# A hybrid decoder block on one core: the merge's second operands split when they are loaded, its sums kept behind them, and scan transpositions placed inside the first product

## The chip, the core and the metric

The kernel runs on one core of one Trainium2 chip. The metric is the device time of one execution in microseconds (us). Before the change three runs took 1994.7, 1999.32 and 2001.35 us; their median is 1999.32 us.

## What is computed

The reference is a decoder block in float32 with 1024 tokens and 1024 channels. Two branches run in parallel: an attention with forget gates (FoX, 8 heads) and a gated delta rule (GDN, a chunked scan, 8 heads). Their outputs pass a projection each, are weighted by sigmoid gates and added, then follow an output projection, a gated feed-forward part with a short convolution, and a norm. The lines that matter here:

```python
o = gated_delta_rule(q, k, v, g, beta)
o = rmsnorm(o, gdn_norm[l]) * jax.nn.silu(gz.reshape(B, S, GDN_HEADS, GDN_HEAD_V))
y_gdn = o.reshape(B, S, GDN_V_WIDTH)

y = (jax.nn.sigmoid(gate_fox) * jnp.einsum('bse,ed->bsd', y_fox, w_branch_fox[l])
     + jax.nn.sigmoid(gate_gdn) * jnp.einsum('bse,ed->bsd', y_gdn, w_branch_gdn[l]))
h = h + jnp.einsum('bsd,de->bse', y, w_out[l])
```

## The kernel before

**Products in split precision.** A large product is not run on float32 operands. Each operand is split (`split`, L106 and L107) into a high part, a cast by ACT (`oh`, `yh`), and a low part, source minus high part, subtracted by DVE or POOL (`ol`, `yl`). `half_product` (L1654) then runs three matmuls for a pair: high by high, high by low, low by high. In `merge_split` (L1494) the weights become `oh` and `ol`, the activations `yh` and `yl`.

**The stages.** Projections of the input come first (to about 780 us). Then `mix` (L1285) runs the attention and the scan side by side: the attention's generator `fox` is advanced step by step, and two streams of scan heads (even heads, odd heads) are advanced in between. `merge` (L1513) follows, for branch 0 (FoX) and branch 1 (GDN), then the output projection (`mix_out`), the feed-forward part (`ffn_up`, `ffn_down`) and the output.

**The end of a scan head.** `columns(h)` (L1383) is a generator. Its first step loads the head's gate `sgz` and lets POOL scale the scan's output `so` (L1391 to L1396). Its next two steps each transpose four 128x128 blocks on PE (L1401), let ACT evict them into `yge` (L1405, for heads 6 and 7), let POOL multiply by the gate (L1406) and store the result in `ygd` (L1409). For head 6, the last of the even stream, these steps run inside the scan's end; head 7 is scaled last, and its transpositions stand in the middle of the merge's first product.

**The merge.** Each branch is one 1024x1024x1024 product, run as seven half-size products (a Strassen-Winograd scheme, the table `plan`, L1595). Each has four rounds k = 0 to 3, with 12 matmuls in a round. Rounds 0 and 1 run round by round, over the four column blocks i; rounds 2 and 3 then run block by block, so that the blocks end one after the other, and `after` works on each. The first product (n = 0) has operands `a11` and `b11`, which are split during the attention's end (`merge_first`, L1501). The second (n = 1) has `a12` and `b21`, loaded early into free buffers of the scan's inputs (`br_raw2`; in the trace they are named after these buffers: `skt`, `saq`, `sqd`, `skT` for k = 0 to 3). The splits of the second product are issued after `evicted`, the last eviction of `columns` (L1617). Each round of it also forms sums for later products (`sums2`, L1544): `b12 - b11` and `b22` minus that on DVE, `b22 - b12` on POOL. After each finished block, `gate` (L1522) loads the gate (L1525) and DVE weights the block with it (L1528).

**Order and buffers.** PE's order is the program's order. SP, ACT, DVE and POOL are ordered by a scheduler that works on a timeline of its own, except where the program pins an operation (`keep_in_program_order`) or ties it to another (`issue_after`). Each engine then works strictly in its order. Buffers are tiles of pools that are opened over memory that earlier pools gave up; an operation on a tile waits for the last use of what lay there. The gates' tiles `g` (four of 512 columns) lie in the pool `br2`, which `merge_gates` (L472) opens when the pool `so` (scan output, `sgz`, `yge`) is closed.

Of the kernel before, what the change touches and what calls it, by code (L numbers as in the profile page):

```python
# [9 lines left out]
F32 = mybir.dt.float32  # L10
# [57 lines left out]
def finish(gen):  # L68
    for _ in gen:
        pass  # L70
# [17 lines left out]
class Block:  # L88
# [322 lines left out]
    def run(self):  # L411
# [5 lines left out]
        with ExitStack() as ctx:  # L417
# [54 lines left out]
            def merge_gates():  # L472
                so.close()
                self.br.append(pool(bs, "br2"))

            def merge_second():
                si.close()
# [807 lines left out]
    def mix(self, fp, pool, before_last):  # L1285
        tc, nc, a = self.tc, self.nc, self.a
        self.yf_d, self.yg_d = ([self.dr.tile([P, S], F32, name=f"{n}{h}") for h in range(H)] for n in ("yfd", "ygd"))
        if True:
# [94 lines left out]
            def columns(h):  # L1383

                o, sumo = outs.pop(h)
                gz = self.so.tile([P, S], F32, tag="sgz", bufs=1, name="sgz")
                nc.sync.dma_start(gz, self.gz_d[h])
                f = self.rq[:, h, :]
                g_ = nc.gpsimd
                rs = self.so.tile([P, NB], F32, tag="srs", bufs=2, name="srs")  # L1390
                g_.tensor_tensor(rs, sumo, f, ALU.mult)  # L1391
                g_.tensor_tensor(rs, rs, f, ALU.mult)
                self.rsqrt(rs, rs, 1.0 / P, EPS)
                g_.tensor_tensor(rs, rs, f, ALU.mult)
                for sl in (slice(0, 4), slice(4, 8)):
                    g_.tensor_tensor(o[:, sl], o[:, sl], rs[:, sl].unsqueeze(2).to_broadcast([P, 4, P]), ALU.mult)  # L1396
                yield
                for g in range(2):
                    ps = self.small()
                    for j in range(4):  # L1400
                        nc.tensor.transpose(ps[:, j * P:(j + 1) * P], o[:, 4 * g + j, :], self.ident)  # L1401
                    y = self.so.tile([P, 512], F32, tag="yge", bufs=2, name="yge")
                    sl = slice(g * 512, (g + 1) * 512)
                    if h >= H - 2:
                        self.evicted = nc.scalar.activation(y, ps, AF.Copy, scale=self.gn[:, 0:1]).ins  # L1405
                        nc.gpsimd.tensor_tensor(y, y, gz[:, sl], ALU.mult)  # L1406
                    else:
                        nc.vector.scalar_tensor_tensor(y, ps, self.gn[:, 0:1], gz[:, sl], op0=ALU.mult, op1=ALU.mult)
                    nc.sync.dma_start(self.yg_d[h][:, sl], y)  # L1409
                    yield  # L1410
# [3 lines left out]
            def stream(s):  # L1414

                prev = iter(())
                for h in range(s, H, 2):
                    finish(preps.pop(h))
                    for i, _ in enumerate(scan(h)):
                        if i in (1, 6, 8):  # L1420
                            take(prev, 1)
                        if h + 2 < H and i in (14, 18, 21):
                            if i == 14:
                                preps[h + 2] = prep(h + 2)
                            take(preps[h + 2], 1)
                        yield
                    finish(prev)
                    prev = columns(h)
                if s == 0:
                    merge_loads(self.br_raw2, ("a12", "b21"), ("skt", "saq", "sqd"))  # L1430
                for _ in range(0 if s else 3):
                    take(prev, 1)
                    yield
                self.last.append(prev)

            def merge_loads(raw, names, tags):
# [33 lines left out]
            before_last()  # L1470
            for s in streams:
                finish(s)
            take(self.last[1], 1)


# [37 lines left out]
    def merge(self, gates_pool, second_pool):  # L1513
# [18 lines left out]
        for br in range(2):  # L1532
# [11 lines left out]
            def sums2(k):  # L1544
                b11, b12, b22 = (get(n, k) for n in ("b11", "b12", "b22"))
                t1 = b11 if br else temp(0, "b11")
                v.tensor_tensor(t1, b12, b11, subtract)
                b11 = blocks["b11", k] = t1
                t2 = blocks["t2", k] = temp(1, "t2")
                v.tensor_tensor(t2, b22, b11, subtract)  # L1550
                g.tensor_tensor(b12, b22, b12, subtract)
                if br == 0:

                    get("s2", k)
# [50 lines left out]
            for n, (wn, yn, tag, sums, after) in enumerate(plan):  # L1605
                fresh = n in (0, 1, 3)
                if fresh:
                    banks[tag] = [self.mm.tile([P, 512], F32, tag=tag, bufs=4, name=tag) for _ in range(4)]
                ps, last = banks[tag], []
                for k in range(4):  # L1610
                    if br == n == 0:
                        blocks["b11", k] = self.br_raw[k][:, 512:1024]
                        blocks["a12", k], blocks["b21", k] = (self.br_raw2[k][:, 512 * j:512 * (j + 1)] for j in range(2))
                        w, y = self.br_first.pop(0)
                    elif br == 0 and n == 1:

                        with self.tc.issue_after(self.evicted):  # L1617
                            w, y = self.merge_split(get(wn, k), get(yn, k), v)
                    else:
                        w, y = self.merge_split(get(wn, k), get(yn, k), v)  # L1620
                    if sums:
                        sums(k)
                    if k < 2:
                        for i in range(4):
                            self.half_product(ps[i], i, k, 4, y, w, fresh)
                    else:
                        last.append((k, 4, y, w, fresh))
                if br == n == 0:
# [466 lines left out]
```

## Time and profile before

| what | value |
| --- | --- |
| median of three runs | 1999.32 us |
| the profiled execution's own time | 2001.23 us |
| its span, first to last instruction | 1999.3 us |
| mean granted TensorE clock | 0.990 |
| PE busy, share of the span | 1923.4 us, 96% |
| DVE busy, share of the span | 1495.2 us, 75% |
| first, second and third product of the merge start at | 1072.1, 1084.1 and 1103.1 us |

A row of the timeline gives the start and the length in us, then the engine (PE matrix products, DVE, ACT and POOL the three vector engines, SPq SP's DMA issues), the line of the code, the operation, the tile written and the tiles read, the shape, and the count of merged instructions. Behind it, in brackets, stands how long the engine was idle just before, and what ended that. The lines of the code before are used throughout; behind the change they are higher by 2 to 6.

### The profile page before, as it was taken

The numbers are of one execution on the slowest core, as the hardware profiler recorded it, in microseconds if no ns is written. First come the engines' busy times: TensorE is split into PE (matmuls) and PEld (weight loads), VectorE is DVE, ScalarE is ACT, GpSimd is POOL, SyncE is SP. The second block draws the span as 40 slices with busy tenths as digits, with TensorE's granted clock in tenths as the row PEclk, the third lists the DMA queues.
The fourth block names the chain that finished last, engine by engine and source line by source line (L and its number), as shares of the span: only waits on it lengthen the run. The fifth ranks groups of instructions, "written<-read, shape, count | busy, mean of one in ns | idle before, by whom it ended". The sixth has DMA issues, their size and how long they took to land. (4 is left out here: it accounts for less than half of the span.)

```text
span 1999.3 us, 29171 instructions
## 1 busy us (share of the span) xinstructions
PE 1923.4 (96%) x9674; PEld 1609.2 (80%) x9674; DVE 1495.2 (75%) x2552; ACT 1067.3 (53%) x2383; POOL 938.7 (47%) x785
## 2 busy tenths in 40 slices
PE   8999999999999999899997999999999999999998
PEld 8988887788887877788886887877788888877886
DVE  6948888867999974487887797667876766778535
ACT  5436777763333455476765443466655555553234
POOL 2845656565554555465554033145656666530012
PEclk9999999999999999999999999999999999999999
DMA  5234556565323376767665933564433344378654
GB/s 170 92 108 160 176 190 185 182 217 195 122 99 107 111 227 252 216 222 233 212 215 172 317 107 121 183 228 153 152 117 132 132 132 137 103 247 322 222 191 162
DMA packets 191607, 350.88 MB, mean 176 GB/s; under 512 B 50784, under 2 KB 79712, under 8 KB 191456
## 3 DMA queue, kind: packets, MB, share of 16 engines
q1 hardware_dynamic: 189728, 344.04, 51.7%
q10 hardware_dynamic: 1728, 4.98, 0.6%
q8 instruction: 76, 1.25, 0.3%
q14 instruction: 75, 0.61, 0.1%
HBM read 232.76 MB, written 116.20 MB: 175 GB/s over the span
## 5 line engine op out<-in xcount | busy, mean ns | idle before, releaser
L107 POOL TENSOR_TENSOR ol<-ws,oh 128x512 fp32r<-128x512 f32 x212 | 290.6, 1373 | 217.2 <-ACT oh L106 206.9
L107 POOL TENSOR_TENSOR ol<-wr,oh 128x512 fp32r<-128x512 f32 x165 | 230.5, 1399 | 275.6 <-ACT oh L106 254.1
L106 ACT CAST oh<-ws 128x512 fp32r<-128x512 f32 x212 | 131.1, 618 | 176.6 <-PE mm L159 158.0
L205 DVE TENSOR_TENSOR ws<-wr 128x512 f32<-128x512 f32 x106 | 103.3, 974 | 98.8 <-DMA wr<-in_w_up_dram 73.1
L106 ACT CAST oh<-wr 128x512 fp32r<-128x512 f32 x201 | 121.4, 615 | 104.3 <-PE mm L159 72.0
L390 DVE SCALAR_TENSOR_TENSOR cv<-c,fw,cv 128x512 f32<-128x512 f32 (+2 forms) x176 | 127.5, 748 | 9.8 <-ACT cv L385 8.4
L390 DVE SCALAR_TENSOR_TENSOR cv<-c,cw,cv 128x511 f32<-128x511 f32 (+2 forms) x144 | 105.9, 747 | 7.8 <-ACT cv L385 6.3
L1044 DVE TENSOR_TENSOR invt<-invz 128x399 f32<-128x399 f32 (+50 forms) x114 | 95.0, 847 | 0.3
L264 ACT COPY x<-mm 128x512 f32<-128x512 f32 x158 | 91.8, 581 | 3.2 <-PE mm L159 3.2
L159 PE MATMUL mm<-b22h,oh 128*128 128x512 f32 x216 | 85.7, 397 | 5.9 <-ACT x L264 5.9
L159 PE MATMUL mm<-bt1h,oh 128*128 128x512 f32 x216 | 85.6, 396 | 4.3 <-ACT x L264 4.2
L159 PE MATMUL mm<-bt4h,oh 128*128 128x512 f32 x216 | 85.5, 396 | 3.4 <-DVE c L311 3.4
L107 DVE TENSOR_TENSOR ol<-wd,oh 128x512 fp32r<-128x512 f32 x66 | 45.5, 692 | 56.5 <-ACT oh L106 56.5
L159 PE MATMUL mm<-b11h,oh 128*128 128x512 f32 x216 | 85.9, 398 | 1.0 <-ACT oh L106 1.0
L159 PE MATMUL mm<-b11h,ol 128*128 128x512 f32 x216 | 85.9, 398 | 0.7 <-POOL ol L107 0.7
L159 PE MATMUL mm<-bt4l,oh 128*128 128x512 f32 x216 | 86.1, 399 | 0.0
L159 PE MATMUL mm<-b11l,oh 128*128 128x512 f32 x216 | 85.9, 398 | 0.0
L159 PE MATMUL mm<-b21l,oh 128*128 128x512 f32 x216 | 85.8, 397 | 0.0
L159 PE MATMUL mm<-b22l,oh 128*128 128x512 f32 x216 | 85.6, 396 | 0.0
L159 PE MATMUL mm<-bt2l,oh 128*128 128x512 f32 x216 | 85.1, 394 | 0.3 <-DVE bt2l L107 0.3
L159 PE MATMUL mm<-b21h,oh 128*128 128x512 f32 x216 | 85.2, 394 | 0.0
L159 PE MATMUL mm<-bt4h,ol 128*128 128x512 f32 x216 | 85.2, 394 | 0.0
(455 smaller groups left out, 6371.5 us busy)
## 6 DMA issues: line engine op xcount, KB each, us to landing
wr<-in_w_up_dram SPq DMA_DIRECT2D x43, 512.0 KB, 3.7
wr<-in_w_gdn_dram SPq DMA_DIRECT2D x24, 512.0 KB, 3.7
wr<-in_w_out_dram SPq DMA_DIRECT2D x24, 512.0 KB, 4.0
s<-z SPq DMA_DIRECT2D x44, 256.0 KB, 3.7
wd<-in_w_down_dram SPq DMA_DIRECT2D x44, 256.0 KB, 5.8
b22h<-s SPq DMA_DIRECT2D x44, 256.0 KB, 3.0
b22l<-s SPq DMA_DIRECT2D x44, 256.0 KB, 3.3
s<-hy SPq DMA_DIRECT2D x41, 256.0 KB, 3.0
```

The lines of the kernel that those rows point to most:

```text
L106: cast = nc.scalar.copy(hi, src)
L107: (lo_eng or nc.vector).tensor_tensor(lo, src, hi.bitcast(F32), ALU.subtract)
L159: self.nc.tensor.matmul(ps, lhs[:, sl], rhs[:, k, :], start=(first and k == 0 and i == 0), stop=(k == 3 and i == 2), skip_group_check=True)
L205: v.tensor_tensor(t, x, y, op)
L264: nc.scalar.copy(t, x)
L390: nc.vector.scalar_tensor_tensor(t[:, lo:], c[:, 512 * j + lo - s:512 * (j + 1) - s], w[:, n - 1 - s:n - s], t[:, lo:], op0=ALU.mult, op1= ...
L1044: nc.vector.tensor_tensor(tv, z[:, m:n, 0:n].to_broadcast([P, r, n]), z[:, m, c0:c1].unsqueeze(2).to_broadcast([P, r, n]), ALU.mult))
```

## The change

It has four parts.

1. Head 6's transpositions leave the scan. The even stream now only takes the first step of `columns` at its end (the scaling). The two transposing steps are taken inside the merge's first product, after blocks 1 and 3 of its first two rounds; head 7's stay where they were, behind round 1.
2. The second product's four splits are issued together, ahead of its rounds, and no longer tied to `evicted`.
3. In branch 0 the sums `b12 - b11` of DVE are pinned into program order, which is behind those splits.
4. A tile `gap` of 6 x 512 columns is put in front of the gates' tiles in their pool, so that these lie 12 KB further on. Nothing reads or writes it.

```diff
             def merge_gates():
                 so.close()
                 self.br.append(pool(bs, "br2"))
+
+                self.br[2].tile([P, 6 * 512], F32, name="gap")
...
                     if h >= H - 2:
-                        self.evicted = nc.scalar.activation(y, ps, AF.Copy, scale=self.gn[:, 0:1]).ins
+                        nc.scalar.activation(y, ps, AF.Copy, scale=self.gn[:, 0:1])
                         nc.gpsimd.tensor_tensor(y, y, gz[:, sl], ALU.mult)
...
                 if s == 0:
                     merge_loads(self.br_raw2, ("a12", "b21"), ("skt", "saq", "sqd"))
-                for _ in range(0 if s else 3):
+                if s == 0:
                     take(prev, 1)
-                    yield
                 self.last.append(prev)
...
                 t1 = b11 if br else temp(0, "b11")
-                v.tensor_tensor(t1, b12, b11, subtract)
+                ins = v.tensor_tensor(t1, b12, b11, subtract)
+                if br == 0:
+
+                    self.tc.keep_in_program_order(ins)
...
                 ps, last = banks[tag], []
+                early = []
+                if br == 0 and n == 1:
+                    early = [self.merge_split(get(wn, k), get(yn, k), v) for k in range(4)]
                 for k in range(4):
                     if br == n == 0:
...
                         w, y = self.br_first.pop(0)
-                    elif br == 0 and n == 1:
-
-                        with self.tc.issue_after(self.evicted):
-                            w, y = self.merge_split(get(wn, k), get(yn, k), v)
                     else:
-                        w, y = self.merge_split(get(wn, k), get(yn, k), v)
+                        w, y = early.pop(0) if early else self.merge_split(get(wn, k), get(yn, k), v)
                     if sums:
                         sums(k)
                     if k < 2:
                         for i in range(4):
                             self.half_product(ps[i], i, k, 4, y, w, fresh)
+                            if br == n == 0 and i % 2:
+                                take(self.last[0], 1)
```

What this makes of the order on the engines is shown at three places. Numbers behind a name tell its buffers apart.

DVE at the merge's start, before: `b11` written is the sum `b12 - b11`, `t2` the sum from it, `ol` and `yl` are the low parts of the second product's weights and activations (`skt` for k = 0, `saq` for k = 1, `sqd` for k = 2, `skT` for k = 3).

```order
L1547 TENSOR_TENSOR b11_12180<-b12_12074,skT_11623 128x512
L1547 TENSOR_TENSOR b11_12207<-b12_12076,skt_11626 128x512
L1547 TENSOR_TENSOR b11_12234<-b12_12078,saq_11629 128x512
L1547 TENSOR_TENSOR b11_12249<-b12_12080,sqd_11632 128x512
L107 TENSOR_TENSOR ol_12173<-skt_11889,oh_12172 128x512
L1550 TENSOR_TENSOR t2_12182<-b22_12082,b11_12180 128x512
L107 TENSOR_TENSOR yl_12177<-skt_11889,yh_12176 128x512
L107 TENSOR_TENSOR ol_12200<-saq_11892,oh_12199 128x512
L1550 TENSOR_TENSOR t2_12209<-b22_12084,b11_12207 128x512
L107 TENSOR_TENSOR yl_12204<-saq_11892,yh_12203 128x512
```

The same place of DVE after the change:

```order
L107 TENSOR_TENSOR yl_12178<-skt_11889,yh_12177 128x512
L107 TENSOR_TENSOR yl_12186<-saq_11892,yh_12185 128x512
L107 TENSOR_TENSOR yl_12194<-sqd_11895,yh_12193 128x512
L107 TENSOR_TENSOR yl_12202<-skT_12004,yh_12201 128x512
L1549 TENSOR_TENSOR b11_12205<-b12_12056,skT_11623 128x512
L107 TENSOR_TENSOR ol_12174<-skt_11889,oh_12173 128x512
L1555 TENSOR_TENSOR t2_12207<-b22_12064,b11_12205 128x512
L1549 TENSOR_TENSOR b11_12224<-b12_12058,skt_11626 128x512
L107 TENSOR_TENSOR ol_12182<-saq_11892,oh_12181 128x512
L1555 TENSOR_TENSOR t2_12226<-b22_12066,b11_12224 128x512
```

The four activation splits now stand first and one sum stands ahead of the first weight split, where four stood. Behind these rows follow, after the change, two more `b11` and two more `t2`, then `ol` of `sqd` and `ol` of `skT`, then `ol` of the third product's first `s2`; before it was the same set in another order, and the same `ol` of `s2` behind it.

ACT from the attention's last output on, before: `yge` is the eviction of four transposed blocks, `z` the copy of a finished block of the first product.

```order
L1249 COPY ye_12019<-ya_11839 128x512
L1379 ACTIVATE sjk_12016,sumo_11254<-so_11253 128x128
L1251 DMA yfd7_8364<-ye_12019 128x512
L1405 ACTIVATE yge_12123<-ms_12118,gn_542 128x512
L1405 ACTIVATE yge_12132<-ms_12127,gn_542 128x512
L106 CAST oh_12172<-skt_11889 128x512
L106 CAST yh_12176<-skt_11889 128x512
L106 CAST oh_12199<-saq_11892 128x512
L106 CAST yh_12203<-saq_11892 128x512
L106 CAST yh_12230<-sqd_11895 128x512
L106 CAST yh_12245<-skT_12022 128x512
L1566 COPY z00_12044<-a_12090 128x512
```

ACT at the same place after the change:

```order
L1253 DMA yfd7_8364<-ye_12001 128x512
L1407 ACTIVATE yge_12087<-ms_12082,gn_542 128x512
L106 CAST yh_12177<-skt_11889 128x512
L106 CAST yh_12185<-saq_11892 128x512
L106 CAST yh_12193<-sqd_11895 128x512
L106 CAST yh_12201<-skT_12004 128x512
L106 CAST oh_12173<-skt_11889 128x512
L1407 ACTIVATE yge_12102<-ms_12097,gn_542 128x512
L106 CAST oh_12181<-saq_11892 128x512
L1571 COPY z00_12026<-a_12072 128x512
L1407 ACTIVATE yge_12123<-ms_12118,gn_542 128x512
```

The second product's activation casts now stand behind the first eviction of head 6 (`yge_12087`) where they stood behind both of head 7. POOL's order changes with it: head 6's first gating (L1406) now stands behind the small steps and ahead of the scaling (L1396) of head 7, head 6's second behind that scaling, and head 7's two gatings behind the four subtractions `b22 - b12` (L1551), where all four gatings stood ahead of these. On SP the eight loads of `b12` and `b22` follow directly on the loads of `skT`; the load of `sgz` for head 7 and three of the four stores of `yge` stand behind those and behind six loads of weight sums.

DVE in `ffn_down`, at its first product, before; the scheduler's order there differs too, though no code of it was touched. `wd` written is a sum of weights that waits for a load, `ol` and `yl` are the low parts of round 6 and those after it.

```order
L2027 TENSOR_SCALAR nfin_18709<-nfin_18709 128x1024
L107 TENSOR_TENSOR yl_18753<-hr_18750,yh_18752 128x512
L1878 TENSOR_TENSOR wd00_0_18238<-wd0512_0_18742,wd00_0_18238 128x512
L107 TENSOR_TENSOR ol_18747<-wd00_6_18744,oh_18746 128x512
L1878 TENSOR_TENSOR wd00_1_18277<-wd0512_1_18770,wd00_1_18277 128x512
L107 TENSOR_TENSOR yl_18779<-hr_18750,yh_18778 128x512
L107 TENSOR_TENSOR ol_18775<-wd00_7_18772,oh_18774 128x512
L1878 TENSOR_TENSOR wd00_2_18305<-wd0512_2_18796,wd00_2_18305 128x512
L107 TENSOR_TENSOR yl_18807<-hr_18804,yh_18806 128x512
L1878 TENSOR_TENSOR wd00_3_18656<-wd0512_3_18824,wd00_3_18656 128x512
L107 TENSOR_TENSOR ol_18801<-wd00_8_18798,oh_18800 128x512
```

The same place after the change:

```order
L107 TENSOR_TENSOR yl_18754<-hr_18751,yh_18753 128x512
L2033 TENSOR_SCALAR nfin_18710<-nfin_18710 128x1024
L107 TENSOR_TENSOR ol_18748<-wd00_6_18745,oh_18747 128x512
L1884 TENSOR_TENSOR wd00_0_18239<-wd0512_0_18743,wd00_0_18239 128x512
L107 TENSOR_TENSOR yl_18780<-hr_18751,yh_18779 128x512
L1884 TENSOR_TENSOR wd00_1_18278<-wd0512_1_18771,wd00_1_18278 128x512
L107 TENSOR_TENSOR ol_18776<-wd00_7_18773,oh_18775 128x512
L1884 TENSOR_TENSOR wd00_2_18306<-wd0512_2_18797,wd00_2_18306 128x512
L107 TENSOR_TENSOR yl_18808<-hr_18805,yh_18807 128x512
L107 TENSOR_TENSOR ol_18802<-wd00_8_18799,oh_18801 128x512
L1884 TENSOR_TENSOR wd00_3_18657<-wd0512_3_18825,wd00_3_18657 128x512
```

The low part `ol` of round 8 stands ahead of the sum `wd00_3` where it stood behind it, and that of round 6 ahead of `wd00_0`. On ACT the load of `nfin` is issued two casts later.

## The prediction

> **What bounds the kernel now.** I read the page, then a table of windows over the merge, then PE, DVE and POOL in order of time through its first two products.
>
> ```profile
> span 1999.3 us, 29171 instructions
> ...
> PE 1923.4 (96%) x9674; PEld 1609.2 (80%) x9674; DVE 1495.2 (75%) x2552; ACT 1067.3 (53%) x2383; POOL 938.7 (47%) x785
> ```
>
> PE is busy for 96% of the span, so an edit that removes no matmul can only win PE's gaps and its slow stretches. The windows (busy us and count for each engine, granted clock, DMA share, GB/s) show where they lie:
>
> ```profile
> 1060.00:1066.00 6.00, 2.46 (x17) 1.81 (x15) 4.48 (x9) 3.58 (x11) 4.40 (x7) 1.00 0.27 94
> ...
> 1084.00:1090.00 6.00, 0.48 (x3) 0.05 (x1) 6.00 (x6) 1.76 (x4) 4.88 (x3) 0.80 0.72 270
> 1090.00:1096.00 6.00, 5.92 (x17) 4.72 (x18) 6.00 (x12) 1.14 (x2) 0.00 (x0) 0.63 0.00 0
> ...
> 1120.00:1140.00 20.00, 20.00 (x88) 16.19 (x87) 12.97 (x21) 10.34 (x19) 0.00 (x0) 1.00 1.04 383
> ```
>
> From 1120 on PE is full, so whatever the merge's start wins reaches the end. Before it PE stands twice, and once its clock falls to 0.63:
>
> ```profile
> 1065.60 0.66 PE L1401 MATMUL ms<-ident,so 128*128 128x128 f32 x4 [3.54 <-POOL so L1396]
> ...
> 1072.10 0.74 PE L1659 MATMUL a<-yp,oh 128*128 128x512 f32 x2 [0.68 <-ACT ye L1249]
> ...
> 1077.72 1.03 PE L1401 MATMUL ms<-ident,so 128*128 128x128 f32 x8
> ...
> 1084.08 0.40 PE L1659 MATMUL b<-yh,oh 128*128 128x512 f32 x1
> 1090.08 0.80 PE L1659 MATMUL b<-yl,oh 128*128 128x512 f32 x1 [5.60 <-DVE yl L107]
> ...
> 1091.10 0.63 PE L1659 MATMUL b<-yh,oh 128*128 128x512 f32 x1
> 1091.53 0.63 PE L1659 MATMUL b<-yl,oh 128*128 128x512 f32 x1
> ...
> 1094.72 0.40 PE L1659 MATMUL b<-yh,oh 128*128 128x512 f32 x1
> 1094.95 0.40 PE L1659 MATMUL b<-yl,oh 128*128 128x512 f32 x1
> ...
> 1103.12 0.40 PE L1659 MATMUL a<-yh,oh 128*128 128x512 f32 x1
> ```
>
> The first product starts at 1072.10, the second at 1084.08, the third at 1103.12. A matmul takes 0.23 us (1094.72 to 1094.95) and 0.43 while slow (1091.10 to 1091.53). The second product's 48 matmuls need 11.2 us, so of its 19.0 us 5.6 are the stall and some 2.0 the slow clock.
>
> ```profile
> 1067.90 1.00 DVE L1510 TENSOR_TENSOR ol<-sqd,oh 128x512 fp32r<-128x512 f32 x1
> ...
> 1079.19 1.82 DVE L1547 TENSOR_TENSOR b<-b,skT 128x512 f32<-128x512 f32 x1 [9.36 <-DMA b<-yfd]
> ...
> 1086.02 1.74 DVE L107 TENSOR_TENSOR ol<-skt,oh 128x512 fp32r<-128x512 f32 x1
> ...
> 1089.35 0.68 DVE L107 TENSOR_TENSOR yl<-skt,yh 128x512 fp32r<-128x512 f32 x1
> 1089.95 0.68 DVE L107 TENSOR_TENSOR ol<-saq,oh 128x512 fp32r<-128x512 f32 x1
> ...
> 1094.77 0.68 DVE L107 TENSOR_TENSOR ol<-skT,oh 128x512 fp32r<-128x512 f32 x1
> ```
>
> ```profile
> 1064.50 2.04 POOL L1396 TENSOR_TENSOR so<-so,srs 128x512 f32<-128x512 f32 x2
> 1067.06 1.30 POOL L1406 TENSOR_TENSOR yge<-yge,sgz 128x512 f32<-128x512 f32 x1 [0.52 <-ACT yge L1405]
> ...
> 1072.43 0.20 POOL L1391 TENSOR_TENSOR srs<-sumo,rq 128x8 f32<-128x8 f32 x1 [1.49 <-ACT sjk L1379]
> ...
> 1075.29 2.04 POOL L1396 TENSOR_TENSOR so<-so,srs 128x512 f32<-128x512 f32 x2
> 1079.17 2.99 POOL L1406 TENSOR_TENSOR yge<-yge,sgz 128x512 f32<-128x512 f32 x2 [1.84 <-DMA b<-yfd]
> 1082.12 6.75 POOL L1551 TENSOR_TENSOR b<-b,b 128x512 f32<-128x512 f32 x4
> ```
>
> DVE is what the second product waits for: idle for 9.36 us, then four sums ahead of any split. Until POOL's last subtraction ends (1088.87) each of DVE's operations takes about 1.75 us, afterwards one starts every 0.60. POOL's take 1.69 there (6.75/4) against 1.30. The two take turns: 0.60 for DVE, 1.09 for POOL.
>
> **The change, step by step.**
>
> *Start of the first product.* Head 6's transpositions leave the scan. Gone from PE are the 3.54 and 0.8 for eight transpositions (1077.72's eight, started within 0.8): 4.3 us. Next late is DVE: the last two splits of the attention's end, L1510 for `sqd`, move up into POOL's scaling of 1064.50 and stand ahead of an attention split that PE needs. If each waits for one half of the scaling (1.02), 4.3 - 2.0 = 2.3 us remain; if not, 4.3. I take 2.3, since the split at 1067.90 did wait for the gating at 1067.06 (1.00 for 0.68). Start: 1069.8.
>
> [...]
>
> *The first product.* It took 12.0 us with eight transpositions and takes 12.8 with sixteen. After 24 matmuls and eight transpositions (5.6 + 0.8) PE wants head 7's, at 1076.2. POOL's small steps for it took 2.9 (1072.43 to 1075.29), now from 1070.1 to 1073.0; then come one gating, now ahead of the scaling, and two halves (1.3 + 2.04), with DVE's splits between (two or three at 0.6, less the pause between operations, 0.2 each): 1077.5. The second half is wanted at 1076.6, so PE waits about 0.9. The second product starts at 1069.8 + 12.8 + 0.9 = 1083.5, only 0.6 earlier.
>
> *Operands of the second product.* ACT's four casts stand behind the first eviction, which needs head 6's transpositions (1.4 into the product), so the first `yl` comes at 1073.0, not when its load has landed. From there DVE has 16 operations: four `yl`, then sums and `ol`. POOL offers ten in that time (four gatings and four subtractions at 1.09, two scalings at 0.8): 10.3 us. The last `ol` but one, k = 2, is the fifteenth: 1073.0 + 14 x 0.60 + 10.3 = 1091.7, ready at 1092.4. `ol` of k = 0 is the sixth and is ready at about 1081.6, before 1083.5; that of k = 1 is the ninth, ready at 1086.7 where PE wants it at 1083.5 + 14 x 0.233 = 1086.8. So the 5.60 goes, but at matmul 27 (1089.6) PE waits until 1092.4: 2.8 to 3.0 us for `ol` of k = 2. Another 22 matmuls (5.1) and the third product starts at 1097.7. Against 1103.12 that is **-5.4**; the old order, worked through in the same way, comes out 0.1 early, so -5.3.
>
> *The clock after that stall.* An earlier stall of that size:
>
> ```profile
> 782.43 0.39 PE L1194 MATMUL ms<-kl,qh 128*128 128x256 f32 x1 [2.76 <-POOL kl L1142]
> ...
> 783.98 0.63 PE L159 MATMUL mm<-b11h,ol 128*128 128x512 f32 x1
> 784.40 0.63 PE L159 MATMUL mm<-b11h,oh 128*128 128x512 f32 x1
> ...
> 786.54 0.63 PE L159 MATMUL mm<-b11h,ol 128*128 128x512 f32 x1
> ```
>
> Seven matmuls at 0.43 follow it: 7 x 0.195 = 1.4 us. After the 3.54 at 1065.60 none do (they stand 0.23 apart). I take **+1.4**, bounds 0 and 2.0 (what followed the 5.60).
>
> [...]
>
> *Moved without a price.* SP's loads of `b12` and `b22`, and how long a gate's load takes to land:
>
> ```profile
> 1072.83 5.92 SPq L1484 DMA_DIRECT2D b<-yfd  x8
> ```
>
> ```profile
> DMA to landing us min/median/max: 2.5/3.0/4.8
> ```
>
> The eight loads no longer queue behind head 6's stores, which wait for POOL; they can go once the scan's buffers are free, some 5 us earlier, so DVE's 9.36 us wait for them goes too (its sums now come at 1079 anyway). Head 7's `sgz` load and its stores lie behind them, waiting for POOL; behind those stand the gates' loads, whose buffers moved onto `sgz` and `yge`. POOL's last gating ends at about 1089.4, its store lands at about 1092.4 if it takes the 3.0 of a gate's load. The gates' loads wait anyway for the split of the first `s2`, the operation after the last `ol`, at about 1093.7. That covers it by 1.3 us: 0, at worst +0.5. Without that cover each us is one on L1528 and on the splits behind it in DVE's queue.
>
> *The last stage.* There the order shifts by itself, as the scheduler works it out anew. DVE, PE and ACT before:
>
> ```profile
> 1791.90 0.69 DVE L2027 TENSOR_SCALAR nfin<-nfin 128x1024 f32<-128x1024 f32 x1 [3.08 <-DMA nfin<-in_norm_final_dram]
> ...
> 1801.29 0.69 DVE L1878 TENSOR_TENSOR wd<-wd,wd 128x512 f32<-128x512 f32 x1 [0.98 <-DMA wd<-in_w_down_dram]
> 1801.89 0.68 DVE L107 TENSOR_TENSOR ol<-wd,oh 128x512 fp32r<-128x512 f32 x1
> ```
>
> ```profile
> 1800.01 0.62 ACT L106 CAST oh<-wd 128x512 fp32r<-128x512 f32 x1 [8.31 <-DMA wd<-in_w_down_dram]
> ```
>
> ```profile
> 1802.63 0.50 PE L1659 MATMUL a<-ol,yh 128*128 128x512 f32 x1 [1.45 <-DVE ol L107]
> ```
>
> `ol` of k = 8 now precedes the sum that waits for its load, so it need not start at 1801.89 but once its high part is cast, at 1800.7: **-1.2**, bounds +1 (`nfin`, loaded two casts later, holds DVE longer than its 3.08) and -1.45 (the whole wait).
>
> *Sum*, against the profiled execution's 2001.23 (span 1999.3): 2001.23 - 5.3 + 1.4 - 1.2 = 1996.1. The median lies 1.9 below that execution, so 1994.2, or 0.26% under 1999.32.
>
> **Rivals.** *The clock stays full*, as after 1065.60: -5.3 - 1.2 = -6.5, 1992.8. For it: one stall of 3.54 without harm; against: 782.43. Chance 0.22.
>
> *The scalings exclude no split*: the first product starts at 1067.8 and ends without a wait at 1080.6; DVE's last splits come 3.6 earlier, the wait for k = 2 is 2.1, the third product starts at 1093.9: -9.2 - 1.2, about 1989. Against it 1067.90, which though was beside a gating. Chance 0.12.
>
> *Slower: the gates wait for the scan's last store.* If head 7's store of `yge` lands at L, the second gate lands 3.0 later and L1528 runs then; four operations behind it stands the split that the third product wants for k = 2, ready at L + 6.1. PE wants it at 1104.7 (1099.1 after the slow clock, plus 24 matmuls), so from L = 1098.6 on each us costs one, and such a stall the slow clock again (2.0). At L = 1103 that is +4.4 + 2.0 against -5.1: 2000.6. It turns slower from L = 1101.7. For it: the gates' loads have these waits now, and two casts, one load and one store of head 7 stand one behind the other. Against it: my 1092.4. Chance 0.05.
>
> *The splits gain nothing* because DVE is as late as before (`ol` of the last k at 1094.77): only start and `yl` are won, 2 to 3 us, 1996 to 1997. Chance 0.11.
>
> **How the numbers follow.** The forecast, 0.50: 1994.2, its own range 1992 to 1997. A measurement of this kernel (1994.7 to 2001.35 in three runs) can tell about 0.3%, 6 us, from no change, and the forecast lies just inside. Faster by more: nearly all of the second rival, somewhat over half of the first, and what of the forecast the spread carries over, 0.40. Slower by more needs the slow rival and the spread, 0.05. The rest, 0.55. The range 1990.0 to 1998.8 leaves out most of the second rival and the slow one.
>
> **What would show it.** Right: no PE wait on POOL's `so` before the first product; its start 2 to 4 us earlier; `yl` from about 1073; no 5.60 stall, in its place 2 to 4 us inside the second product for `ol`, with DVE at 1.7 beside POOL; the third product 4 to 5 us earlier. Wrong: a first product that ends later than 1084, an `ol` of k = 0 after the second product's start, a wait of DVE for gates above 1 us, or a last stage that shifts by more than 2 us.

## The result: 0.993 of the time before, a larger gain than forecast

Six runs of the changed kernel have a median of 1985.36 us (1982.76 to 1988.31), six of the kernel before 1999.16 us. The ratio is 0.9931, interval 0.9911 to 0.9951: 13.8 us less, where the forecast said 5.1 and its range ended at 1990.0. A second set gave 0.9944 (0.9926 to 0.9961), some 11.2 us less (0.0056 of 1998.2, the median of before over that set). The sign and, in sum, the merge's start came as forecast; a gain of 4 us at the other end of the merge, which the forecast set at 0, did not.

### The profile after

The first lines of the page:

```profile
span 1986.4 us, 29173 instructions
...
PE 1923.4 (97%) x9674; PEld 1610.1 (81%) x9674; DVE 1490.3 (75%) x2552; ACT 1066.8 (54%) x2383; POOL 940.8 (47%) x785
```

PE is busy for the same 1923.4 us, and its granted clock is 0.989 for 0.990: what this profile is shorter by is waiting. PE in order of time, from the attention's last score matmul (1044.12, called A below; it lies ahead of all that the change touches) to the third product:

```profile
1044.12 0.40 PE L1197 MATMUL ms<-kh,ql 128*128 128x512 f32 x1
...
1063.56 0.43 PE L1223 MATMUL ya<-pl,vh 128*128 128x256 f32 x1 [1.77 <-DVE pl L107]
...
1066.15 1.22 PE L1665 MATMUL a<-yp,oh 128*128 128x512 f32 x2 [0.68 <-ACT ye L1251]
...
1074.73 1.03 PE L1403 MATMUL ms<-ident,so 128*128 128x128 f32 x8
...
1081.09 0.40 PE L1665 MATMUL b<-yh,oh 128*128 128x512 f32 x1
...
1088.59 0.50 PE L1665 MATMUL b<-yh,ol 128*128 128x512 f32 x1 [0.95 <-DVE ol L107]
...
1090.27 0.50 PE L1665 MATMUL b<-yh,ol 128*128 128x512 f32 x1 [0.71 <-DVE ol L107]
...
1096.32 0.39 PE L1665 MATMUL a<-yh,oh 128*128 128x512 f32 x1
```

The 3.54 us for `so` and the 5.60 for `yl` are gone. In their place stand 1.77 for the attention's last `pl`, and 0.95 and 0.71 for `ol`. Head 7's eight transpositions (1074.73) waited for nothing. DVE at the same place:

```profile
1060.75 0.97 DVE L1512 TENSOR_TENSOR ol<-sqd,oh 128x512 fp32r<-128x512 f32 x1
1061.65 1.52 DVE L1512 TENSOR_TENSOR yp<-sqd,yp 128x512 fp32r<-128x512 f32 x1
1063.10 0.41 DVE L107 TENSOR_TENSOR pl<-ms,ph 128x256 fp32r<-128x256 f32 x1
1071.20 1.38 DVE L107 TENSOR_TENSOR yl<-skt,yh 128x512 fp32r<-128x512 f32 x1 [7.70 <-ACT yh L106]
...
1077.70 0.68 DVE L107 TENSOR_TENSOR ol<-skt,oh 128x512 fp32r<-128x512 f32 x1
...
1086.76 1.78 DVE L107 TENSOR_TENSOR ol<-sqd,oh 128x512 fp32r<-128x512 f32 x1
1088.46 1.75 DVE L107 TENSOR_TENSOR ol<-skT,oh 128x512 fp32r<-128x512 f32 x1
```

The prediction's working goes from the third product straight to the last stage. Between them, at the end of the merge, where the output projection (`mm`) begins, a wait has gone that it does not mention. PE, ACT and POOL there, before:

```profile
1237.46 0.40 PE L1659 MATMUL b<-yh,ol 128*128 128x512 f32 x1
1241.62 1.22 PE L1651 MATMUL mm<-oh,yh 128*128 128x512 f32 x2 [3.76 <-ACT yh L106]
```

```profile
1241.06 0.51 ACT L106 CAST yh<-z 128x384 fp32r<-128x384 f32 x1 [8.55 <-POOL z L1530]
```

```profile
1235.66 5.36 POOL L1530 TENSOR_TENSOR z<-z,g 128x512 f32<-128x512 f32 x4 [3.29 <-DVE g L1528]
```

And after:

```profile
1229.19 0.39 PE L1657 MATMUL mm<-oh,yh 128*128 128x512 f32 x1
1231.25 0.50 PE L1657 MATMUL mm<-oh,yh 128*128 128x512 f32 x1 [1.67 <-DVE g L1530]
```

```profile
1223.51 0.51 ACT L106 CAST yh<-z 128x384 fp32r<-128x384 f32 x1
```

```profile
1227.18 5.63 POOL L1532 TENSOR_TENSOR z<-z,g 128x512 f32<-128x512 f32 x4 [3.28 <-DVE g L1530]
```

The cast of the projection's first operand waited 8.55 us, until POOL's last addition of a gate had ended (1241.02). Its source had been finished earlier: after the change the same cast runs 3.7 us before POOL's last four additions begin, and waits for nothing. PE stood 3.76 us and went on at half clock (granted 0.50 from 1241.62 to 1244.60, 1.22 us for two matmuls); now it stands 1.67 and goes on at full clock (granted 1.00 from 1231.25 to 1234.00, 0.62 us for two).

### The profile page after: what moved, and what is told of

It reads as the page before. It is cut to its first block, busy times and chain, and to the rows that moved or that the text cites. A ratio compares the mean times of both kernels' runs of the same rounds, so it can differ in the third digit from the quotient of the medians.

```text
span 1986.4 us, 29173 instructions
## 1 busy us (share of the span) xinstructions
PE 1923.4 (97%) x9674; PEld 1610.1 (81%) x9674; DVE 1490.3 (75%) x2552; ACT 1066.8 (54%) x2383; POOL 940.8 (47%) x785
## 5 line engine op out<-in xcount | busy, mean ns | idle before, releaser
L205 DVE TENSOR_TENSOR ws<-wr 128x512 f32<-128x512 f32 x106 | 96.0, 906 | 107.2 <-DMA wr<-in_w_up_dram 72.7
L159 PE MATMUL mm<-bt1l,oh 128*128 128x512 f32 x216 | 85.4, 395 | 0.0
```

The source lines that it names most:

```text
L159: self.nc.tensor.matmul(ps, lhs[:, sl], rhs[:, k, :], start=(first and k == 0 and i == 0), stop=(k == 3 and i == 2), skip_group_check=True)
L205: v.tensor_tensor(t, x, y, op)
```

## The experiments

Each kernel left one profile. Since one program's executions differ by some us before A already (A lies between 1042.41 and 1048.87 in all profiles), the table counts from A: to the first product, from start to start of the products, from the third product to the output projection, and from there to PE's last matmul. The ratio is to the kernel before on the same chip.

| kernel | A to 1st | 1st to 2nd | 2nd to 3rd | 3rd to projection | to the last matmul | ratio (95%) |
| --- | --- | --- | --- | --- | --- | --- |
| before | 23.61 | 11.98 | 19.04 | 138.50 | 749.70 | |
| before, again | 23.59 | 11.98 | 18.84 | 136.63 | 749.64 | 1.0003 (0.9988-1.0018) |
| gap alone | 24.97 | 11.95 | 18.89 | 132.54 | 750.65 | 0.9979 (0.9961-0.9997) |
| transpositions alone | 21.27 | 18.21 | 14.44 | 136.45 | 751.73 | 0.9989 (0.9971-1.0006) |
| splits and pin alone | 25.20 | 11.94 | 13.56 | 137.82 | 749.29 | 0.9968 (0.9953-0.9983) |
| changed, no gap | 21.26 | 13.24 | 14.96 | 137.05 | 749.91 | 0.9971 (0.9956-0.9986) |
| changed | 22.03 | 14.94 | 15.23 | 132.87 | 749.22 | 0.9931 (0.9911-0.9951) |
| changed, again | 21.55 | 15.38 | 13.20 | 134.55 | 747.13 | 0.9944 (0.9926-0.9961) |
| gap of 2 | 21.27 | 14.43 | 13.76 | 134.56 | 747.05 | 0.9937 (0.9918-0.9956) |
| gap of 4 | 21.27 | 14.47 | 13.62 | 134.56 | 751.25 | 0.9949 (0.9930-0.9967) |
| `pl` first | 19.27 | 13.25 | 16.96 | 132.51 | 750.04 | 0.9957 (0.9940-0.9973) |
| early casts | 21.30 | 14.46 | 11.34 | 142.14 | 749.77 | 0.9966 (0.9952-0.9980) |
| early casts, pinned sums | 21.26 | 14.39 | 11.73 | 134.15 | 748.70 | 0.9940 (0.9921-0.9958) |
| both orders | 19.26 | 12.92 | 17.95 | 132.54 | 750.00 | 0.9947 (0.9928-0.9966) |

### The two kernels again

No edit.

> The kernel before, unchanged, a second time: a control for what differs between two executions of one program. Between the two profiles the program is the same up to about 1060 us, and yet the changed one is 2.9 us ahead there, 4.0 of it at one wait of PE for a load (sx, at 831.89). If that is the change of a day and not of the kernel, this run shows some other size of that wait (0.5 to 4 us) and a time within 0.3% of before. The theory that buffers decide what came after the merge expects PE's wait of 3.8 us for yh ahead of the output projection here again, to a tenth, and matmuls of the merge 0.233 us apart; the rival, that all this is chance, expects other numbers in both places.

> The changed kernel a second time, with its own profile: 0.993 of before again. Buffers theory: no wait for yh ahead of the output projection (a wait of 1.7 us one matmul later instead), matmuls of the merge 0.229 us apart, both as in the first profile. Chance: these two move by themselves, and the wait for sx at about 832 us is as often 4 us as 1.

The wait for `sx` is chance: 4.02 and 2.35 us in before's two profiles, 0.91 and 5.59 in the changed kernel's.

```profile
829.36 1.84 PE L1334 MATMUL ms<-sx,sat 64*64 64x64 f32 x16 [2.35 <-DMA sx<-xd]
```

```profile
830.84 1.40 PE L1336 MATMUL ms<-sx,sat 64*64 64x64 f32 x11 [5.59 <-DMA sx<-xd]
```

So what the changed kernel is ahead at A in its first profile says nothing. The wait for `yh` ahead of the projection is not chance: 3.78 in before again, none after.

```profile
1237.48 1.22 PE L1651 MATMUL mm<-oh,yh 128*128 128x512 f32 x2 [3.78 <-ACT yh L106]
```

The 0.233 us between matmuls was chance, against what the buffers theory expected: before's second profile ran this stretch at 0.229, as all other profiles do, and so 1.9 us faster (136.63 for 138.50) with the same instructions. The second profile is therefore the one to compare with.

### The gap alone, and all but the gap

```diff
                 self.br.append(pool(bs, "br2"))
+                self.br[2].tile([P, 6 * 512], F32, name="gap")
```

> The kernel before with the tile gap alone; no instruction moves, but the gates' tiles lie 12 KB further on. As my forecast had it, this gives 0 to +0.5 us. Buffers theory: before, the first gate tiles lie where the output projection's first yh is written, so that cast waits for POOL's last addition of a gate; with the gap it does not, so the wait of 3.76 us and its slow clock go, a wait of 1.7 with slow clock comes: -3.5 to -4.5 us (0.998), and up to -2.5 more if the 0.229 us between the merge's matmuls comes with the gap too. The merge's start stays as before (third product at about 1103 us, 5.6 us wait for yl).

> The changed kernel without gap: new order, old place of the gates' tiles. As my forecast had it: the third product about 4 us earlier than before and nothing further, 0.998 of before. Buffers theory: the same 4 us at the merge, then the wait of 3.8 us for yh again at the end of the merge, so 4 to 6 us slower than the changed kernel. Rival (the new order is what removes that wait, since all splits and gates come earlier): the wait is gone here too and the time is that of the changed kernel.

The gap alone takes 4.1 us from one stretch, third product to projection (136.63 to 132.54), and leaves the products before it alone (it reaches the first one 1.4 us later by a chance of the clock, shown in the last section). The whole ratio, 0.9979, is 4.2 us (0.6 to 7.8). Without the gap the wait is back:

```profile
1232.79 1.22 PE L1655 MATMUL mm<-oh,yh 128*128 128x512 f32 x2 [3.79 <-ACT yh L106]
```

and the new order earns 0.9971, 5.8 us (2.8 to 8.8). 4.2 and 5.8 make 10.0, against 11.2 and 13.8 measured for both, inside both intervals. The rival, that the new order removes the wait, falls: PE's wait for `yh` is 3.76 to 3.79 us in all five profiles without the gap, whatever the order, and in none of the nine with it.

### Where the gap puts the gates

The edit is the 6 of the gap, changed to 2 and to 4.

> The changed kernel with a gap of 2 x 512 columns in place of 6: the gates' tiles then lie at bytes 121888 to 130080 of a partition, over the output projection's yl (121696 to 124768) but no longer over its yh (118624 to 121696). Buffers theory: the cast to yh is free at once, but the split to yl waits for POOL's last addition of a gate, so PE gets two products of four matmuls and then stands 2.5 to 4 us; as slow as the changed kernel without gap or up to 1.5 us better: p. e. 0.996 of before. Rival (only yh, which ACT writes, matters, since DVE has other work ahead of yl anyway): as fast as the changed kernel, 0.994.

> The changed kernel with a gap of 4 x 512 columns: the gates' tiles lie at bytes 125984 to 134176, behind both yh and yl of the output projection and still over its norm's tiles (from 124768 on), as with 6. Buffers theory: the wait of PE ahead of the output projection is the 1.7 us of the changed kernel, and the time the changed kernel's, within the spread (0.994). Rival (what matters is that the gates' tiles lie over the scan's sgz and yge, 130976 to 139232, whose stores delay the gates' loads): the gates' loads start at other times, and the time differs by 1 us or more from the first gates on.

As the built programs lay them out, the four gate tiles lie from byte 117792 on before the change and the last gate in the one at 119840 to 121888; the projection's two `yh` lie at 118624 to 121696, both over it. With a gap of 2 the last gate lies at 123936, over a `yl` only; with 4 and 6 behind all four. The times of all three agree (0.9937 with 2, 0.9949 with 4, 0.9931 and 0.9944 with 6), so with 2 the rival holds: only `yh` matters. Why `yl` costs nothing is seen in DVE and POOL with a gap of 2:

```profile
1232.96 0.69 DVE L1530 SCALAR_TENSOR_TENSOR g<-g,b 128x512 f32<-128x512 f32 x1
1233.57 0.55 DVE L107 TENSOR_TENSOR yl<-z,yh 128x384 fp32r<-128x384 f32 x1
1234.03 2.39 DVE L107 TENSOR_TENSOR ol<-wr,oh 128x512 fp32r<-128x512 f32 x2
1236.35 0.55 DVE L107 TENSOR_TENSOR yl<-z,yh 128x384 fp32r<-128x384 f32 x1
```

```profile
1229.63 5.64 POOL L1532 TENSOR_TENSOR z<-z,g 128x512 f32<-128x512 f32 x4 [3.29 <-DVE g L1530]
```

DVE weights the last block itself just ahead of `yl`, so it comes to the first `yl` late anyway, and to the second after POOL has ended (1235.27). ACT, without the gap, had nothing else to do and stood the 8.55 us. With a gap of 2 the gates lie over neither the scan's `sgz` nor its `yge` (130976 to 139232), with 4 over `sgz` alone, with 6 over both; that all are as good shows that these places play no part.

### Transpositions alone, splits alone

```diff
-                for _ in range(0 if s else 3):
+                if s == 0:
                     take(prev, 1)
-                    yield
...
                             self.half_product(ps[i], i, k, 4, y, w, fresh)
+                            if br == n == 0 and i % 2:
+                                take(self.last[0], 1)
```

> Before with part 1 alone: head 6's transpositions inside the first product, the second product's splits still tied to the last eviction, sums not pinned, no gap. What the scheduler makes of it: on DVE all eight sums (b11, t2) now stand ahead of the second product's first split, where four stood. Theory of parts (each part is worth what the prediction gave it, by itself): the start of the first product 2 us earlier, the second product as late as before, 1 to 2 us faster, 0.999. Rival (parts 1 and 2 only work together, since DVE's order hangs on both): the start is 2 us earlier, but DVE's first split comes after eight sums at 1.75 us beside POOL, so PE stands 6 to 9 us in the second product; third product no earlier than before, time 1.000 to 1.002.

The other kernel has the early splits and the pin, and none of this:

```diff
-                v.tensor_tensor(t1, b12, b11, subtract)
+                ins = v.tensor_tensor(t1, b12, b11, subtract)
+                if br == 0:
+                    self.tc.keep_in_program_order(ins)
...
+                if br == 0 and n == 1:
+                    early = [self.merge_split(get(wn, k), get(yn, k), v) for k in range(4)]
```

> Before with parts 2 and 3 alone: early splits and pinned sums, transpositions of head 6 in the scan as before, no gap. Theory of parts: the first product starts as before, the second product takes some 15 us in place of 18.9, because one sum and not four stands ahead of the second weight split; third product 3 to 4 us earlier, 0.998. Rival (the splits gain only if the transpositions leave the scan, since the casts stand behind head 6's second eviction and head 7's): the 5.6 us wait shrinks by under 2 us.

The transpositions alone bring the start forward by 2.3 us and lose it: the casts, tied to the last eviction, come when the product ends, and PE stands.

```profile
1084.83 0.80 PE L1660 MATMUL b<-yh,oh 128*128 128x512 f32 x1 [3.48 <-ACT yh L106]
1086.72 0.79 PE L1660 MATMUL b<-yl,oh 128*128 128x512 f32 x1 [1.09 <-DVE yl L107]
```

The rival held in kind (third product hardly earlier: 53.92 us behind A, before 54.6 and 54.4), but not its DVE: the eight sums were done in time, and DVE then stood 3.46 us for the cast. The time, 0.9989, can't tell the two theories apart. The splits alone take 5.3 us off the second product (18.84 to 13.56), more than expected, and 0.9968 is as good as splits and transpositions together (0.9971). So in this change the splits earn the order's gain; that the transpositions add anything isn't shown. The start of 25.20 is a chance of the clock, shown in the last section.

### Three attempts at what still stands

`pl` first puts the first product's last operand split behind the attention's last `pl`:

```diff
-                    elif half and i in (0, 2, 3, 5):
+                    elif half and i in (0, 2, 3, 6):
                         self.merge_first(len(self.br_first))
```

> The changed kernel with the attention's end in another order on DVE: the last two splits of the first product's operands (sqd, k = 3) behind the attention's last pl instead of ahead of it. In every profile with the transpositions moved, PE stands 1.76 us for that pl, which waits for these two splits beside POOL's scaling (0.97 and 1.52 us for 0.68), and in four of five matmuls at 0.43 us follow for 2 to 6 us. Theory of the prediction's first step (the two splits cost what they take beside POOL): the wait goes, the first product starts 1.8 us earlier, 19.5 in place of 21.3 us behind the attention's last score matmul; with the clock's part 2 to 4 us in all at the start of the second product. Rival (the end of the attention hangs on ACT and PE as well, the two splits then stand beside the next scaling): under 0.5 us. What is won at the start can be lost at the second product, since DVE's and POOL's work for it starts with head 6's transpositions and not earlier than these.

The 1.76 us for `pl` went, and the start came 2.0 us earlier (19.27). It is lost again in the second product:

```profile
1080.69 0.40 PE L1665 MATMUL b<-yh,ol 128*128 128x512 f32 x1
1085.15 0.51 PE L1665 MATMUL b<-yh,oh 128*128 128x512 f32 x1 [4.07 <-ACT yge L1407]
...
1086.20 0.59 PE L1665 MATMUL b<-yl,oh 128*128 128x512 f32 x1
...
1089.57 0.44 PE L1665 MATMUL b<-yh,oh 128*128 128x512 f32 x1
```

```profile
1084.41 0.69 ACT L1407 ACTIVATE yge<-ms,gn 128x512 f32<-128x512 f32 x1 [4.49 <-DMA ygd<-yge]
```

The transposed blocks lie in the banks of the second product (`self.ms_tag = "b"`). Its fourth block gets its bank when ACT has evicted head 7's last four blocks, and ACT waited 4.49 us for a buffer `yge` that a store still read. This chain is not in the prediction, though part of it shows in the changed order too (2.09 us for `yge` without the gap).

The other two bring the second product's activation casts ahead of head 6's first eviction:

```diff
+                if br == n == 0:
+                    ys = []
+                    for src in (r[:, 512:1024] for r in self.br_raw2):
+                        parts = [self.br[0].tile([P, 512], F32R, tag=t, bufs=4, name=t) for t in ("yh", "yl")]
+                        self.cast = nc.scalar.copy(parts[0], src).ins
+                        v.tensor_tensor(parts[1], src, parts[0].bitcast(F32), subtract)
+                        ys.append(parts)
+                elif br == 0 and n == 1:
+                    early = [(self.operand(get(wn, k), v), ys.pop(0)) for k in range(4)]
...
+                        with self.tc.issue_after(self.cast):
+                            nc.scalar.activation(y, ps, AF.Copy, scale=self.gn[:, 0:1])
```

> The changed kernel with the second product's activation casts (yh) ahead of head 6's first eviction on ACT, so that DVE's first yl no longer waits for that eviction (7.70 us idle in the changed kernel). The scheduler then puts all eight splits ahead of the eight sums on DVE. Theory (the second product waits for DVE's late start, as the prediction had it: first yl behind the eviction): yl from 4 us earlier, all four ol as soon as ACT has cast their oh, no wait in the second product (1.7 us and its slow clock go), 2 to 3 us faster at the third product. Rival (DVE's work is only moved): ol of k = 2 and 3 wait for casts behind the first product's end, DVE stands for them and the eight sums come late, so the third product waits for yl of t2 instead: 0 or up to 3 us slower than the changed kernel at its end.

The second product then has no wait (11.34), and the rival holds as well: DVE stood for the casts of `oh`, the sums came late, and the third product paid.

```profile
1078.15 0.69 DVE L107 TENSOR_TENSOR ol<-sqd,oh 128x512 fp32r<-128x512 f32 x1 [5.03 <-ACT oh L106]
```

```profile
1091.67 0.50 PE L1673 MATMUL a<-yl,oh 128*128 128x512 f32 x1 [1.76 <-DVE yl L107]
1100.84 0.50 PE L1673 MATMUL a<-yl,oh 128*128 128x512 f32 x1 [3.39 <-DVE yl L107]
```

With the sums pinned between the splits:

```diff
+                    for k in range(4):
+                        if k > 1:
+                            sums(k)
+                        w = [self.wt.tile([P, 512], F32R, tag=t, bufs=self.nw, name=t) for t in ("oh", "ol")]
+                        nc.scalar.copy(w[0], get(wn, k))
+                        self.tc.keep_in_program_order(
+                            v.tensor_tensor(w[1], get(wn, k), w[0].bitcast(F32), subtract))
+                        if k < 2:
+                            sums(k)
```

> As the run with the early casts, and DVE's order pinned: sums of k = 0 and 1 each behind its ol, sums of k = 2 ahead of ol of k = 2. Theory: DVE uses the time in which it was idle, ol of k = 2 is ready before PE wants it, and the sums are early enough for the third product: second product 11.1 us without a wait, third product at 13.5 + 11.2 us behind the first's start, 3 us faster than the changed kernel, 0.9925 of before. [...]

> The two orders together: pl ahead of the last splits of the first product's operands, early casts, sums pinned between the splits. If both theories hold, the third product starts 5 to 6 us earlier than in the changed kernel, counted from the attention's last score matmul, and the time is 0.991 to 0.992 of before. If the start is not bound by the two splits, this is no better than the run with early casts and pinned sums.

Early casts with pinned sums reach the third product 47.4 us behind A and the projection 181.5; the changed kernel needed 50.1 and 184.7 in its second profile. By the trace that is about the 3 us expected; the ratio, 0.9940, can't be told from the changed kernel's 0.9931 and 0.9944. Both orders together are no better: PE stood 2.46 and 1.57 us for head 7's evictions.

## Why the prediction was wrong, point by point

**The start of the first product** was right: 2.3 us, 21.27 for 23.6. Its reason was right in kind: the two splits beside POOL's scaling (1060.13 to 1062.62 in the changed kernel's first profile) took 0.97 and 1.52 us where one alone takes 0.68, and with `pl` ahead of them the start moved another 2.0. Of these 2.0, which the prediction puts down to the scaling, that is 1.1; the rest fits the time of the splits themselves. The rival in which scalings exclude no split is out.

**The first product** was put at 13.7 us: 12.8 and 0.9 of waiting for head 7's `so`. That wait came in one of the five profiles with this order and the attention's end as in the change, at 0.16 us. The product took 13.24 without slow clock and 14.4 to 15.4 with it. That clock, after a stall of 1.77 us in the attention, was missing from the sum: up to 2 us.

**The second product** was put at 15.6 with the clock and took 13.2 to 15.2. The first `yl` came 3.4 us behind the first product's start without slow clock, as worked out (3.2), and 4.6 to 5.1 with it. From there to the end of `ol` of k = 2 DVE took 17.3 to 17.5 us in all five, where the prediction has 19.4 (1073.0 to 1092.4): by its own sum POOL's turns took some 8.3 us of that, not 10.3. PE's waits were 1.3 to 2.1 us, not 2.8 to 3.0. Without gap all of the wait, with gaps of 2 and 4 a part of it (0.86 and 0.65 us), stood for a bank that ACT had to free and not for `ol`. The clock fell after these waits in two of the five, so the 1.4 for it was no sure term, and the rival in which the clock stays full is not refuted. (A slip of 0.2 in the sum, 1092.4 + 5.1 = 1097.5 and not 1097.7, changes nothing.)

From A to the third product the sum gives 54.6 - 5.3 + 1.4 = 50.7; the five profiles give 49.36 to 52.20, mean 50.1. That it fits so well is partly luck: the first product took 14.5 in the mean for 13.7, the second 14.2 for 15.6.

**The last stage**, -1.2: from `ffn_up`'s last matmul to the third product of `ffn_down` 66.18 and 66.13 us before, 64.38 to 65.31 in the same five, -1.4 in the mean. Right in size, but that `ol` gave only a part: PE's wait in its round was 1.45 and 1.16 us before and is 0.4 to 1.1 in the five; the rest came off the rounds beside it.

**The gates' buffers** are the step that failed. The prediction says of them that a wait is covered, "0, at worst +0.5", and considers only what the moved tiles wait for: POOL's gatings and head 7's stores. That cover held: in the changed kernel's first profile the split of the first `s2` ends at 1091.91 and the first gate's load is issued at 1092.36. But DVE came to the gates before they had landed and waited 0.85 to 1.27 us (0.98 without the gap, so this belongs to the new order); above 1 us this was one of the prediction's signs of being wrong. Where the third product had begun early PE then stood for a split behind them (1.19 and 0.23 us in the second profile):

```profile
1104.85 0.51 PE L1665 MATMUL a<-yl,oh 128*128 128x512 f32 x1 [1.19 <-DVE yl L107]
1106.05 0.51 PE L1665 MATMUL a<-yl,oh 128*128 128x512 f32 x1 [0.23 <-DVE yl L107]
```

But that is not the failure. A buffer has a second neighbour in time, the tile that is laid over it later. Where the gates lie now no cast waits for them; before, the projection's first operand waited for the last of them. That term is -4.1 in the stretch to the projection, and 4.2 us (0.6 to 7.8) in the time of the gap alone; the gap alone and its absence show it. The prediction says "From 1120 on PE is full", and reads that from a window that ends at 1140; the 3.76 us stand at 1241.62 in the same profile.

With it the sum would have been -9.2, 0.9954, inside the second set's interval and 0.0003 above the first's. What is left of 11.2 to 13.8 us can't be told from the spread of the executions.

The rival that was slower, gates that wait for the scan's last store, is out: their loads followed the split, as said. The splits that gain nothing are out too (18.84 to 13.56 us for the second product with splits and pin alone).

## What to carry to other kernels

When a buffer moves, ask two questions: whose last use must end before it is written, and who is written over it next and waits for its last use; the second can lie in another stage, 140 us on. A wait of a cast or load that ends with a later operation than the one that finished its source (here ACT's `yh<-z`, which waited for POOL's last addition, when the `z` that it reads was done) is the sign of such an overlay, and an allocation alone can remove it, with no instruction moved. The names in a trace don't tell it from a wait for the source, since POOL writes `z` as well; the test is to move the tile and nothing else. And test the parts of a change apart: here the gap, and the splits with the pinned sums, gave what can be measured, while the transpositions, which removed a visible wait of 3.54 us, gave nothing that could be.

## What the runs showed of the hardware

**The clock.** Stalls of 1.75 to 1.78 us for `pl` were followed by slow matmuls in seven of the eight profiles that have them, but not at once and not always: the first product took 14.39 to 15.38 us in six of the seven (18.21 in the seventh, a wait of 3.48 us among it) and 13.24 in the eighth. The changed kernel with a gap of 4, PE:

```profile
1064.67 0.38 PE L1223 MATMUL ya<-pl,vh 128*128 128x256 f32 x1 [1.76 <-DVE pl L107]
...
1066.52 0.74 PE L1665 MATMUL a<-yp,oh 128*128 128x512 f32 x2 [0.68 <-ACT ye L1251]
1067.08 0.60 PE L1665 MATMUL a<-yp,ol 128*128 128x512 f32 x1
...
1070.47 0.42 PE L1665 MATMUL a<-yp,ol 128*128 128x512 f32 x1
```

The clock falls at 1067.08, 2.4 us after the stall ended (0.68 us for `ye` stand between), and is back at 1070.47: 3.39 us. In the changed kernel's first profile it falls 0.2 us after the 1.77. After the 4.07 us of the kernel with `pl` first it falls at 1086.20, 1.05 us after the stall, and is back at 1089.57: 3.37. The same 1.75 us stall left the first product's start at full speed in the changed kernel without gap (13.24 in the table). And the 3.54 us for `so`, harmless in both profiles of before, were not so with the gap alone and with splits and pin alone. The latter, PE:

```profile
1065.82 0.66 PE L1401 MATMUL ms<-ident,so 128*128 128x128 f32 x4 [3.53 <-POOL so L1396]
...
1067.10 0.62 PE L1221 MATMUL ya<-pl,vh 128*128 128x512 f32 x1
1067.52 0.63 PE L1221 MATMUL ya<-ph,vl 128*128 128x512 f32 x1
...
1071.07 0.39 PE L1221 MATMUL ya<-pl,vh 128*128 128x512 f32 x1
```

That is why these two reach the first product late (24.97 and 25.20 us behind A). In the first profiles of the kernel before and of the changed one the granted clock is 0.50 in ten stretches each. Within a profile these begin whole multiples of 3.413 us apart, over the whole span, and each but the last, which stands at the run's end, lasts 3.41 or 6.83 us; two of the changed kernel's are 1063.76 to 1070.59 and 1091.07 to 1094.48, their starts 8 x 3.413 us apart. That the slowing after a stall depends on where the stall falls on this grid is an estimate from these rows: after the three stalls timed above the clock fell 0.2, 1.05 and 2.4 us later, each time within one step of the grid. One profile's slow stretch is no term of a sum.

**One execution's pace.** The kernel before ran from the third product to the projection in 138.50 us in one profile and in 136.63 in the next, although PE's waits there were 0.5 us longer in the second. Its matmuls followed at 0.233 us in the first and at 0.229 in the second, as in all the others. What sets this stays open; it is half of what the gap is worth, and seen in a single profile it would have been taken for an effect.
